# Recurrent gates in three float32r passes, and the last scaling on three engines, in a hybrid RG-LRU and GLA layer

## The chip, the cores and the metric

One core of a Trainium2 chip runs the whole layer in one launch. The metric is the device time of one execution in microseconds (us); the median of three is given. A profiled execution also has a span, from its first instruction to its last. Engines are named as the profile names them: PE (TensorE; PEld is its weight load), DVE (VectorE), ACT (ScalarE), POOL (GpSimd), SP (SyncE, which only issues DMAs here). Each takes its instructions strictly in the order of its own queue and waits at the first whose inputs are missing.

## The reference

One decoder layer for 1024 prompt rows and 8 x 4 sample rows that share the weights. The part that the change touches is the RG-LRU's pair of gates, for ten blocks of 128 channels, and the last RMS norm:

```python
xb = xc.reshape(B, T, LRU_BLOCKS, LRU_BW)
r = sigmoid(einsum('btnw,nwv->btnv', xb, wa) + ba)
i = sigmoid(einsum('btnw,nwv->btnv', xb, wx) + bx)
log_a = -LRU_C * softplus(-lam) * r
b = sqrt(-expm1(2.0 * log_a)) * (i * xc)
h = associative_scan(...)            # h_t = exp(log_a_t) * h_(t-1) + b_t
...
y = x * rsqrt(mean(x * x) + EPS) * final_g
```

Around it stand a GEMM into nine column groups, a causal convolution that gives xc, chunked gated linear attention (GLA), two merging projections, an output projection and a SwiGLU feed-forward network. All is float32.

## The kernel before

Activations lie with 128 features on the partitions and tokens along the columns. The tokens are worked in two halves, one after the other: half A is the first 512 prompt rows, half B the other 512 and the 32 sample rows (544 columns, taken as two pieces of 272). Names end in a for half A and in b for half B (g1a, g1b).

Every large GEMM splits its operands into a rounded float32r part (hi, an ACT copy) and the rest (lo, a DVE subtraction), and `gemm` runs three float32r matmuls for each tile of 128 rows: hi x hi, hi x lo, lo x hi (lines 327 to 329). Weights come by `load_w`: SP loads them into a `raw` buffer (three of them), ACT and DVE split them into an `hl` buffer (three). The gates are the exception. `lru_gate` loads 256 columns of gate weights and runs plain float32 matmuls on them and on xc, one per gate and piece (line 832): g1 for r, g2 for i. ACT then makes tanh of both (tr, ti), an exponential la and a tanh from tr, and a square lm; DVE combines them. `lru` runs over five pairs of blocks. For each it emits `lru_x` (projection ux and convolution, giving xc), `lru_g` of the pair before (projection ug and scan), and then `gate(2b)` and `gate(2b + 1)`.

These generators are interleaved with others by hand: the first pair of half A and the first three of half B stand in the GLA stage, the others among the projections gb and pb of `merge_b`. The order in which this emits the work is a priority, from which a scheduler fixes each engine's queue before the run; it also hands out the buffers of a pool as they come free. Matmul results of half A go to six PSUM buffers of one bank, those of half B to three of two banks. The pool of tag `t`, with six buffers, holds xc, tr, ti and the other short-lived rows.

At the end `finish` scales the last 272 columns. `norm` sums the squares by matmuls (nps, line 334), `rsqrt` does Newton steps on DVE, and `spread` makes a row on all partitions by matmuls (rps, line 346), copied from PSUM by ACT (rb, line 349). Eight DVE instructions (line 1054) give y, and each pair of them is followed by a DMA, from SP's and ACT's queues in turn.

Of the kernel before, what the change touches and what calls it, by code (L numbers as in the profile page):

```python
# [7 lines left out]
F32 = mybir.dt.float32  # L8
F32R = mybir.dt.float32r
I32 = mybir.dt.int32  # L10
AF = mybir.ActivationFunctionType
OP = mybir.AluOpType
# [3 lines left out]
P = 128  # L16
D = 1024
KD = 8
# [13 lines left out]
def starts_of(w):  # L32
    return [min(i, w - P) for i in range(0, w, P)]
# [4 lines left out]
V_BA, V_BX, V_LAM, V_GBA, V_GN, V_FG = 114, 124, 134, 144, 148, 156  # L38
# [4 lines left out]
def bc(ap, shape):  # L43
    return ap.to_broadcast(shape)
# [3 lines left out]
def hybrid_layer(ctx, tc, I, O):  # L48
    nc = tc.nc
    pe, act, dve, pool, sp = nc.tensor, nc.scalar, nc.vector, nc.gpsimd, nc.sync  # L50
# [6 lines left out]
    tp = ctx.enter_context(tc.tile_pool(name="tp", bufs=6))  # L57
    axp = ctx.enter_context(tc.tile_pool(name="axp", bufs=2, space=PSUM))

    def S(name, dt=F32):  # L60
        return sbig.tile([P, 2 * 544], dt, tag="S", name=name)

    def T(name, w=544):
        return tp.tile([P, w], F32, tag="t", name=name)

    def ACC(name):
        return tp.tile([P, 544], F32, tag="acc", name="acc" + name, bufs=2)
# [9 lines left out]
    def mm(name):  # L77
        return mmk[1].tile([P, mmk[0], 512], F32, tag="mm", name=name)

    def ax(name):  # L80
        return axp.tile([P, 512], F32, tag="ax", name=name)
# [4 lines left out]
    vec = cp.tile([P, V_TOT], F32, name="vec")  # L86
# [14 lines left out]
    rmask = cp.tile([P, 544], F32, name="rmask")  # L101
# [13 lines left out]
    def load_raw(src, n, name):  # L115
        raw = wp.tile([P, 1024], F32, tag="raw", name=name + "_raw")
        sp.dma_start(raw[:, :n], src)
        return raw
# [39 lines left out]
    def split(dst, src, n):  # L158
        act.activation(dst[:, 0:n], src, AF.Copy)
        dve.tensor_sub(dst[:, n:2 * n], src, dst[:, 0:n].bitcast(F32))  # L160
# [86 lines left out]
    def rsqrt(dst, ssq, n, scale, name):  # L247
        w = cp.tile([P, 3, 16], F32, name="rs_" + name, tag="rs", bufs=2)
        a, t = w[:, 0, :n], w[:, 1, :n]
        yi = cp.tile([P, 16], I32, name="ri_" + name, tag="ri", bufs=2)  # L250
        dve.tensor_scalar(a, ssq, scale, EPS, op0=OP.mult, op1=OP.add)
        dve.tensor_scalar(yi[:, :n], a.bitcast(I32), -0.5, float(0x5F3759DF), op0=OP.mult, op1=OP.add)
        y = yi[:, :n].bitcast(F32)
        for it in range(3):
            dve.scalar_tensor_tensor(t, a, -0.5, y, op0=OP.mult, op1=OP.mult)
            dve.tensor_mul(t, t, y)
            o = dst if it == 2 else w[:, 2, :n]
            dve.scalar_tensor_tensor(o, t, 1.5, y, op0=OP.add, op1=OP.mult)
            y = o

    def drain(g):
        for _ in g:
            pass
# [25 lines left out]
    class Half:  # L289
# [45 lines left out]
                          start=(first and i == 0), stop=(last and i == len(starts) - 1), skip_group_check=True)  # L335


        def spread(s, rstd, w, name):
            starts = starts_of(w)
            nt = len(starts)  # L340
            rps = [ax("rps" + name)] + ([ax("rpt" + name)] if w > HP else [])
            done = 0
            for i, st in enumerate(starts):
                n = st + P - done
                o = rps[0][:, done:done + n] if done < HP else rps[1][:, :n]
                pe.matmul(o, bc(rstd[:, i:i + 1], [P, P]), ident[:, P - n:], start=True, stop=True)
                done += n
            rb = T("rb" + name)
            act.activation(rb[:, :min(w, HP)], rps[0][:, :min(w, HP)], AF.Copy)
            if w > HP:  # L350
                act.activation(rb[:, HP:w], rps[1][:, :w - HP], AF.Copy)
            return rb

        def add_sq(s, acc, x, w, i, name, apart=False):

# [7 lines left out]
            else:  # L363
                acc.append(sq)

        def norm(s, acc, w, box, name):

            starts = starts_of(w)
            nt = len(starts)
            ps = ax("nps" + name)  # L370
            for i, a in enumerate(acc):
                s.ssq_mm(ps, a, starts, 0, i == 0, i == len(acc) - 1)
            rstd = cp.tile([P, 5], F32, name="rstd" + name, tag="rstd", bufs=2)
            rsqrt(rstd[:, :nt], ps[:, :nt], nt, 1.0 / D, name)
            yield 5
            box.append(s.spread(rstd[:, :nt], w, name))
            yield 1.5

        def modulate(s, hs, xs, rb, part, kts, gslot, sh0, name):
# [446 lines left out]
        def lru_gate(s, nb, m, xc):  # L826
            N, n = s.N, f"{s.n}{nb}"
            gw = load_raw(I["lru_w"][nb], 256, "lw" + n)
            g1, g2 = mm("g1" + n), mm("g2" + n)
            for g, c in (g1, 0), (g2, P):  # L830
                for o, w, bank, off in [(0, HP, 0, 0)] if s.hf == 0 else s.parts:
                    pe.matmul(g[:, bank, off:off + w], gw[:, c:c + P], xc[:, o:o + w], start=True, stop=True)
            tr, ti = T("tr" + n), T("ti" + n)
            act.activation(s.sv(tr[:, :N]), s.pv(g1), AF.Tanh, scale=0.5, bias=vh[:, nb:nb + 1])
            act.activation(s.sv(ti[:, :N]), s.pv(g2), AF.Tanh, scale=0.5, bias=vh[:, 10 + nb:11 + nb])
            dve.scalar_tensor_tensor(ti[:, :N], ti[:, :N], 1.0, xc[:, :N], op0=OP.add, op1=OP.mult)
            a = S("la" + n)
            s4 = sp4[:, nb:nb + 1]
            act.activation(a[:, :N], tr[:, :N], AF.Exp, scale=s4, bias=s4)
            act.activation(tr[:, :N], tr[:, :N], AF.Tanh, scale=s4, bias=s4)  # L840
            act.activation(m, a[:, :N], AF.Square)
            dve.scalar_tensor_tensor(m, m, 1.0, tr[:, :N], op0=OP.add, op1=OP.mult)
            return a, ti
# [198 lines left out]
                    s.add_sq(acc, s.x[j][:, s.cols(part)], w, q, "3" + n, back)  # L1042
                yield w * 33 / 2400.0

        def finish(s, part, acc, queues=(pool,)):
            o, w = part[0], part[1]
            box = []
            yield from s.norm(acc, w, box, f"3{s.n}{o}")
            out = O["y" + s.n].rearrange("p (k n) -> p k n", k=KD)
            for j in range(0, KD, 2):  # L1050
                y = S(f"y{s.n}{o}{j}")
                y2 = y[:, :2 * w].rearrange("p (k n) -> p k n", k=2)
                for i in range(2):
                    dve.scalar_tensor_tensor(y2[:, i], s.x[j + i][:, o:o + w], vec[:, V_FG + j + i:V_FG + j + i + 1], box[0][:, :w],
                                             op0=OP.mult, op1=OP.mult)
                    yield 0.0
                (queues[j // 2 % len(queues)]).dma_start(out[:, j:j + 2, o:o + w], y2)

        def back(s):
            s.x, s.h2 = [], []  # L1060
            p0, p1 = s.parts
            a0, a1 = [ACC("20" + s.n)], [ACC("21" + s.n)]
            drain(s.out_proj(p0, a0))
            o1 = s.out_proj(p1, a1)
            next(o1)
            next(o1)
            mix(s.norm2(p0, a0), o1)
            drain(o1)
            s.act = []
            f = s.ffn1_first(p0, EARLY)  # L1070
            next(f)
            next(f)
            mix(s.norm2(p1, a1), f)
            drain(f)
            drain(s.ffn1_first(p1, EARLY))
            drain(s.ffn1(0, EARLY))
            drain(s.ffn2(0, s.whole))
# [30 lines left out]
    A, B = Half(0), Half(1)  # L1108
# [29 lines left out]
    acc = [ACC("3a")]  # L1138
# [7 lines left out]
    p0, p1 = B.parts  # L1146
    a0, a1 = [ACC("30b")], [ACC("31b")]
# [2 lines left out]
    next(dn)  # L1150
    mix(B.finish(p0, a0), dn)
    drain(dn)
    drain(B.finish(p1, a1, (sp, act)))
    mmp.close()


# [92 lines left out]
```

## Time and profile before

| | |
|---|---|
| median of 3 runs | 2042.66 us (2041.41 to 2043.99) |
| profiled execution | 2046.31 us, span 2044.3 us |
| granted TensorE clock, mean | 0.994 |
| PE busy | 2013.5 us, 98% of the span |
| DVE, ACT, POOL busy | 1097.1, 799.2 and 79.5 us |
| gates of half A | 274 to 438 us of the span |
| gates of half B | 1218 to 1394 us of the span |
| last feed-forward matmul ends | about 2031 us |

In rows of the profile, a timeline row has the start in us, the busy time in us, the engine, the line, the output and inputs, and in brackets how long the engine had been idle and for whom it waited. One plain float32 matmul shows as two PE records. A busy time holds the pipeline's depth, so what a matmul costs in a row of equal ones is read from start to start. A row of a stage (from:to) has its length, the busy time and instruction count of PE, PEld, DVE, ACT and POOL, then the granted clock, the DMA share and GB/s.

### The profile page before, as it was taken

To read this page: it belongs to the slowest core of one execution; us is meant where nothing else is said; L and a number is where in the kernel's file an instruction comes from. 1 tells how busy PE (TensorE), PEld (TensorE's weight loads), DVE (VectorE), ACT (ScalarE), POOL (GpSimd) and SP (SyncE) were. 2 spreads that over 40 slices of the span, in tenths; PEclk is the share of its full clock that TensorE was granted. 3 is DMA by queue.
4 is the path that set the end of the run, shared out by engine and by line. 5 is a ranking of instruction groups with operands and counts; after the bars stand their busy time and mean duration, and the time that the engine had idled before them with its cause. 6 is when DMAs were issued, how large, how long until landed. Compare 5 with 4: busy or idle time off the path is not lost. (4 is left out here: it accounts for less than half of the span.)

```text
span 2044.3 us, 31396 instructions
## 1 busy us (share of the span) xinstructions
PE 2013.5 (98%) x13118; PEld 1811.1 (89%) x13118; DVE 1097.1 (54%) x1768; ACT 799.2 (39%) x1117; POOL 79.5 (4%) x131
## 2 busy tenths in 40 slices
PE   8999999999999999999999999999999999999997
PEld 4777787888899888888899999999999999999997
DVE  4647567654358433446473687774334673333346
ACT  3525356644335322233352455553322442222232
POOL 0101000000000000000010111010000000000000
PEclk9999999999999999999999999999999999999998
DMA  8244423332244323232422312323233542232243
GB/s 304 73 157 149 164 68 100 97 103 87 93 152 158 124 81 115 93 138 79 147 67 92 116 53 93 109 88 104 72 93 106 170 137 92 72 105 90 84 120 123
DMA packets 74637, 228.38 MB, mean 112 GB/s; under 512 B 8704, under 2 KB 16768, under 8 KB 74496
## 3 DMA queue, kind: packets, MB, share of 16 engines
q1 hardware_dynamic: 71536, 217.38, 32.1%
q0 software_dynamic: 2416, 8.44, 1.1%
q8 instruction: 103, 1.69, 0.3%
q10 hardware_dynamic: 544, 0.56, 0.1%
q14 instruction: 38, 0.31, 0.0%
HBM read 217.11 MB, written 9.23 MB: 111 GB/s over the span
## 5 line engine op out<-in xcount | busy, mean ns | idle before, releaser
L329 PE MATMUL f3psb<-fab,f3b_hl 128*128 128x272 f32 x352 | 101.6, 289 | 0.0
L327 PE MATMUL f3psb<-fab,f3b_hl 128*128 128x272 f32 x352 | 101.4, 288 | 0.0
L328 PE MATMUL f3psb<-fab,f3b_hl 128*128 128x272 f32 x352 | 101.0, 287 | 0.0
L124 ACT ACTIVATE f3b_hl<-f3b_raw 128x768 fp32r<-128x768 f32 (+1 forms) x45 | 35.7, 793 | 88.7 <-PE f3psb L329 58.3
L327 PE MATMUL f3psa<-faa,f3a_hl 128*128 128x512 f32 x176 | 68.7, 391 | 0.0
L329 PE MATMUL f3psa<-faa,f3a_hl 128*128 128x512 f32 x176 | 68.6, 390 | 0.0
L328 PE MATMUL f3psa<-faa,f3a_hl 128*128 128x512 f32 x176 | 68.6, 390 | 0.0
L327 PEld LDWEIGHTS f3psb<-fab,f3b_hl 128*128 128x128 f32 x352 | 66.5, 189 | 0.0
L329 PEld LDWEIGHTS f3psb<-fab,f3b_hl 128*128 128x128 f32 x352 | 66.3, 188 | 0.0
L328 PEld LDWEIGHTS f3psb<-fab,f3b_hl 128*128 128x128 f32 x352 | 66.2, 188 | 0.0
L125 DVE TENSOR_TENSOR f3b_hl<-f3b_raw,f3b_hl 128x768 fp32r<-128x768 f32 (+1 forms) x45 | 40.1, 892 | 35.1 <-ACT f3b_hl L124 35.0
L124 ACT ACTIVATE f3a_hl<-f3a_raw 128x768 fp32r<-128x768 f32 (+1 forms) x32 | 25.4, 792 | 84.4 <-PE f3psa L329 46.5
L125 DVE TENSOR_TENSOR f3a_hl<-f3a_raw,f3a_hl 128x768 fp32r<-128x768 f32 (+1 forms) x32 | 28.5, 892 | 39.1 <-ACT f3a_hl L124 38.5
L327 PE MATMUL uxpsb<-h1b,uxpsb_hl 128*128 128x272 f32 x160 | 47.6, 298 | 0.1
L329 PE MATMUL uxpsb<-h1b,uxpsb_hl 128*128 128x272 f32 x160 | 46.7, 292 | 0.0
L328 PE MATMUL uxpsb<-h1b,uxpsb_hl 128*128 128x272 f32 x160 | 46.2, 289 | 0.0
L327 PE MATMUL ugpsb<-h1b,ugpsb_hl 128*128 128x272 f32 x160 | 46.2, 289 | 0.0
L329 PE MATMUL ugpsb<-h1b,ugpsb_hl 128*128 128x272 f32 x160 | 46.2, 289 | 0.0
L328 PE MATMUL ugpsb<-h1b,ugpsb_hl 128*128 128x272 f32 x160 | 45.9, 287 | 0.0
L329 PEld LDWEIGHTS f3psa<-faa,f3a_hl 128*128 128x128 f32 x176 | 33.0, 188 | 7.1 <-DVE f3a_hl L125 0.2
L328 PEld LDWEIGHTS f3psa<-faa,f3a_hl 128*128 128x128 f32 x176 | 33.1, 188 | 6.9
L327 PEld LDWEIGHTS f3psa<-faa,f3a_hl 128*128 128x128 f32 x176 | 33.1, 188 | 6.6
(1478 smaller groups left out, 7149.0 us busy)
## 6 DMA issues: line engine op xcount, KB each, us to landing
ada<-in_ada_w SPq DMA_DIRECT2D x48, 512.0 KB, 5.4
f3b_raw<-in_ffn SPq DMA_DIRECT2D x23, 384.0 KB, 3.1
f3b_raw<-in_ffn SPq DMA_DIRECT2D x22, 320.0 KB, 2.8
woa_raw<-in_w_out SPq DMA_DIRECT2D x13, 512.0 KB, 3.4
wob_raw<-in_w_out SPq DMA_DIRECT2D x13, 512.0 KB, 3.3
f3a_raw<-in_ffn SPq DMA_DIRECT2D x16, 384.0 KB, 3.1
uxpsa_raw<-in_w_in SPq DMA_DIRECT2D x10, 512.0 KB, 3.7
ugpsa_raw<-in_w_in SPq DMA_DIRECT2D x10, 512.0 KB, 3.5
```

Of the source, the lines that this page charges most:

```text
L124: act.activation(hl[:, 0, :n], raw[:, :n], AF.Copy)
L125: dve.tensor_sub(hl[:, 1, :n], raw[:, :n], hl[:, 0, :n].bitcast(F32))
L327: pe.matmul(out, wh, x[:, o:o + w], start=st, stop=False)
L328: pe.matmul(out, wh, x[:, N + o:N + o + w], start=False, stop=False)
L329: pe.matmul(out, wl, x[:, o:o + w], start=False, stop=en)
```

## The change

The gates: each block's gate weights are split into gs (hi in columns 0 to 255, lo in 256 to 511), a new tile with one buffer, and xc into xh (ACT) and xl (DVE), tiles of the pool `t`. Each plain matmul becomes three float32r ones: hi x hi, hi x lo, lo x hi. The raw weights are read by the split and no longer by PE.

The end: for the last 272 columns only (`end=True`), two plain matmuls of 512 columns on `rmask` are put between nps and rps; the scaling on DVE reads the row from PSUM (rps) where it read the copy rb; and the last pair of the eight tiles (j = 6) goes first, scaled by the gain on ACT and by rb on POOL.

```diff
@@ -335,7 +335,7 @@
                           start=(first and i == 0), stop=(last and i == len(starts) - 1), skip_group_check=True)
 
 
-        def spread(s, rstd, w, name):
+        def spread(s, rstd, w, name, both=False):
             starts = starts_of(w)
             nt = len(starts)
             rps = [ax("rps" + name)] + ([ax("rpt" + name)] if w > HP else [])
@@ -349,7 +349,7 @@
             act.activation(rb[:, :min(w, HP)], rps[0][:, :min(w, HP)], AF.Copy)
             if w > HP:
                 act.activation(rb[:, HP:w], rps[1][:, :w - HP], AF.Copy)
-            return rb
+            return (rb, rps[0]) if both else rb
 
         def add_sq(s, acc, x, w, i, name, apart=False):
 
@@ -363,7 +363,7 @@
             else:
                 acc.append(sq)
 
-        def norm(s, acc, w, box, name):
+        def norm(s, acc, w, box, name, between=None):
 
             starts = starts_of(w)
             nt = len(starts)
@@ -373,7 +373,9 @@
             rstd = cp.tile([P, 5], F32, name="rstd" + name, tag="rstd", bufs=2)
             rsqrt(rstd[:, :nt], ps[:, :nt], nt, 1.0 / D, name)
             yield 5
-            box.append(s.spread(rstd[:, :nt], w, name))
+            if between is not None:
+                box.append(between())
+            box.append(s.spread(rstd[:, :nt], w, name, between is not None))
             yield 1.5
 
         def modulate(s, hs, xs, rb, part, kts, gslot, sh0, name):
@@ -826,10 +828,19 @@
         def lru_gate(s, nb, m, xc):
             N, n = s.N, f"{s.n}{nb}"
             gw = load_raw(I["lru_w"][nb], 256, "lw" + n)
+            gs = tp.tile([P, 512], F32R, tag="gs", name="gs" + n, bufs=1)
+            split(gs, gw[:, :256], 256)
+            xh, xl = (tp.tile([P, 544], F32R, tag="t", name=u + n) for u in ("xh", "xl"))
+            act.activation(xh[:, :N], xc[:, :N], AF.Copy)
+            dve.tensor_sub(xl[:, :N], xc[:, :N], xh[:, :N].bitcast(F32))
             g1, g2 = mm("g1" + n), mm("g2" + n)
             for g, c in (g1, 0), (g2, P):
+                wh, wl = gs[:, c:c + P], gs[:, 256 + c:256 + c + P]
                 for o, w, bank, off in [(0, HP, 0, 0)] if s.hf == 0 else s.parts:
-                    pe.matmul(g[:, bank, off:off + w], gw[:, c:c + P], xc[:, o:o + w], start=True, stop=True)
+                    out = g[:, bank, off:off + w]
+                    pe.matmul(out, wh, xh[:, o:o + w], start=True, stop=False)
+                    pe.matmul(out, wh, xl[:, o:o + w], start=False, stop=False)
+                    pe.matmul(out, wl, xh[:, o:o + w], start=False, stop=True)
             tr, ti = T("tr" + n), T("ti" + n)
             act.activation(s.sv(tr[:, :N]), s.pv(g1), AF.Tanh, scale=0.5, bias=vh[:, nb:nb + 1])
             act.activation(s.sv(ti[:, :N]), s.pv(g2), AF.Tanh, scale=0.5, bias=vh[:, 10 + nb:11 + nb])
@@ -1042,19 +1053,31 @@
                     s.add_sq(acc, s.x[j][:, s.cols(part)], w, q, "3" + n, back)
                 yield w * 33 / 2400.0
 
-        def finish(s, part, acc, queues=(pool,)):
+        def finish(s, part, acc, queues=(pool,), end=False):
+
             o, w = part[0], part[1]
             box = []
-            yield from s.norm(acc, w, box, f"3{s.n}{o}")
+            yield from s.norm(acc, w, box, f"3{s.n}{o}", s.stay_busy if end else None)
+            rb, rp = box[-1] if end else (box[0], box[0])
             out = O["y" + s.n].rearrange("p (k n) -> p k n", k=KD)
-            for j in range(0, KD, 2):
+            for j in (6, 0, 2, 4) if end else range(0, KD, 2):
                 y = S(f"y{s.n}{o}{j}")
                 y2 = y[:, :2 * w].rearrange("p (k n) -> p k n", k=2)
                 for i in range(2):
-                    dve.scalar_tensor_tensor(y2[:, i], s.x[j + i][:, o:o + w], vec[:, V_FG + j + i:V_FG + j + i + 1], box[0][:, :w],
-                                             op0=OP.mult, op1=OP.mult)
+                    x, g = s.x[j + i][:, o:o + w], vec[:, V_FG + j + i:V_FG + j + i + 1]
+                    if end and j == 6:
+                        act.activation(y2[:, i], x, AF.Copy, scale=g)
+                        pool.tensor_mul(y2[:, i], y2[:, i], rb[:, :w])
+                    else:
+                        dve.scalar_tensor_tensor(y2[:, i], x, g, rp[:, :w], op0=OP.mult, op1=OP.mult)
                     yield 0.0
                 (queues[j // 2 % len(queues)]).dma_start(out[:, j:j + 2, o:o + w], y2)
+
+        def stay_busy(s):
+            ps = mm("busy" + s.n)[:, 0]
+            for _ in range(2):
+                i = pe.matmul(ps, rmask[:, :P], rmask[:, :512], start=True, stop=True, skip_group_check=True)
+                tc.keep_in_program_order(i)
 
         def back(s):
             s.x, s.h2 = [], []
@@ -1150,7 +1173,7 @@
     next(dn)
     mix(B.finish(p0, a0), dn)
     drain(dn)
-    drain(B.finish(p1, a1, (sp, act)))
+    drain(B.finish(p1, a1, (sp, act), True))
     mmp.close()
```

The third pair of gates of half A (blocks 4 and 5), in PE's queue. Before (pbpsa and gbpsa are the GEMMs around it; the numbers tell buffers apart):

```order
L329 MATMUL pbpsa_2595<-yba_2298,pba_hl 128x512
L832 MATMUL g1a_2630<-xca_2434,lwa_raw 128x512
L832 MATMUL g2a_2631<-xca_2434,lwa_raw 128x512
L832 MATMUL g1a_2646<-xca_2548,lwa_raw 128x512
L832 MATMUL g2a_2647<-xca_2548,lwa_raw 128x512
L327 MATMUL gbpsa_2661<-h1a_244,gbpsa_hl 128x512
```

And now:

```order
L841 MATMUL g1a_2681<-xha_2677,gsa_2674 128x512
L842 MATMUL g1a_2681<-xla_2678,gsa_2674 128x512
L843 MATMUL g1a_2681<-xha_2677,gsa_2674 128x512
L841 MATMUL g2a_2682<-xha_2677,gsa_2674 128x512
L842 MATMUL g2a_2682<-xla_2678,gsa_2674 128x512
L843 MATMUL g2a_2682<-xha_2677,gsa_2674 128x512
L841 MATMUL g1a_2708<-xha_2704,gsa_2701 128x512
L842 MATMUL g1a_2708<-xla_2705,gsa_2701 128x512
L843 MATMUL g1a_2708<-xha_2704,gsa_2701 128x512
L841 MATMUL g2a_2709<-xha_2704,gsa_2701 128x512
L842 MATMUL g2a_2709<-xla_2705,gsa_2701 128x512
L843 MATMUL g2a_2709<-xha_2704,gsa_2701 128x512
```

Six matmuls stand where two stood for each block, those of the second block (2708, 2709) directly behind those of the first, and the next GEMM behind both.

The same place in ACT's queue before (gga and yaa belong to `lru_g`, ugpsa_hl is a weight split):

```order
L124 ACTIVATE uxpsa_hl<-uxpsa_raw 128x1024
L851 ACTIVATE gga_2583<-gga_2583 128x512
L159 ACTIVATE yaa_2592<-gga_2583 128x512
L834 ACTIVATE tra_2634<-g1a_2630,vh 128x512
L124 ACTIVATE ugpsa_hl<-ugpsa_raw 128x1024
L835 ACTIVATE tia_2635<-g2a_2631,vh 128x512
L839 ACTIVATE laa_2639<-tra_2634,sp_107 128x512
L834 ACTIVATE tra_2650<-g1a_2646,vh 128x512
L840 ACTIVATE tra_2634<-tra_2634,sp_107 128x512
L841 ACTIVATE lma_2627<-laa_2639 128x512
```

And now, where xha_2704 and gsa_2701 are the second block's:

```order
L862 ACTIVATE gga_2627<-gga_2627 128x512
L834 ACTIVATE xha_2677<-xca_2478 128x512
L159 ACTIVATE yaa_2636<-gga_2627 128x512
L124 ACTIVATE ugpsa_hl<-ugpsa_raw 128x1024
L845 ACTIVATE tra_2689<-g1a_2681,vh 128x512
L846 ACTIVATE tia_2690<-g2a_2682,vh 128x512
L850 ACTIVATE laa_2694<-tra_2689,sp_107 128x512
L159 ACTIVATE gsa_2701<-lwa_raw 128x256
L851 ACTIVATE tra_2689<-tra_2689,sp_107 128x512
L852 ACTIVATE lma_2671<-laa_2694 128x512
L834 ACTIVATE xha_2704<-xca_2592 128x512
L845 ACTIVATE tra_2716<-g1a_2708,vh 128x512
```

The weight split ugpsa_hl has moved ahead of the first block's tra, gs of the second block stands behind the first block's laa, and the second block's xh behind its lma.

The end of POOL's queue, which before ended with the four DMAs:

```order
L1074 DMA out_yb<-yb_18173 128x2x272
L1074 DMA out_yb<-yb_18177 128x2x272
L1074 DMA out_yb<-yb_18181 128x2x272
L1074 DMA out_yb<-yb_18185 128x2x272
L1070 TENSOR_TENSOR yb_18473<-yb_18473,rb3b_18471 128x272 x2
```

The two multiplications are new; in ACT's queue the two products with the gain stand some ten instructions ahead of the end, and the DMA of the j = 6 pair ahead of that of j = 2.

## Prediction

> **What bounds the kernel now.** I read the page's first part, then who waited for whom on PE, then the timeline around the gates, then clock windows.
>
> ```profile
> PE 2013.5 (98%) x13118; PEld 1811.1 (89%) x13118; DVE 1097.1 (54%) x1768; ACT 799.2 (39%) x1117; POOL 79.5 (4%) x131
> PE spsb L620 <- DVE wb L611: 2.3, 1, 2.3
> PE g1b L832 <- DVE mbb L921: 1.0, 1, 1.0
> ```
>
> PE is busy for 98% of the span and its longest wait inside is 2.3 us, so PE's queue is the kernel: matmul time taken away is time won, and each new wait in that queue is time lost, since PE has no slack in which to catch up. ACT and DVE are half empty, but only on average. What matters is when they hand their results to PE. The third pair of gates of half A shows that stage:
>
> ```profile
> 337.16 0.58 ACT L916 ACTIVATE gba<-gbpsa 128x512 f32<-128x512 f32 x1
> 351.73 0.68 DVE L852 SCALAR_TENSOR_TENSOR gga<-gga,ugpsa 128x512 f32<-128x512 f32 x1
> 352.31 1.02 PE L832 MATMUL g1a<-xca,lwa_raw 128*128 128x512 f32 x2
> 352.45 0.69 DVE L867 SCALAR_TENSOR_TENSOR gga<-laa,gga 128x512 f32<-128x512 f32 x1
> 353.17 1.02 PE L832 MATMUL g2a<-xca,lwa_raw 128*128 128x512 f32 x2
> 353.17 0.63 ACT L159 ACTIVATE yaa<-gga 128x512 fp32r<-128x512 f32 x1 [2.10 <-DVE gga L867]
> 353.83 0.69 DVE L160 TENSOR_TENSOR yaa<-gga,yaa 128x512 fp32r<-128x512 f32 x1 [0.69 <-ACT yaa L159]
> 355.42 1.06 ACT L124 ACTIVATE ugpsa_hl<-ugpsa_raw 128x1024 fp32r<-128x1024 f32 x1 [1.05 <-DMA ugpsa_raw<-in_w_in]
> 356.44 0.39 PE L327 MATMUL gbpsa<-h1a,gbpsa_hl 128*128 128x512 f32 x1
> 356.96 0.81 ACT L839 ACTIVATE laa<-tra,sp 128x512 f32<-128x512 f32 x1
> 357.12 0.39 PE L327 MATMUL gbpsa<-h1a,gbpsa_hl 128*128 128x512 f32 x1
> 357.67 0.67 ACT L834 ACTIVATE tra<-g1a,vh 128x512 f32<-128x512 f32 x1
> 358.23 0.81 ACT L840 ACTIVATE tra<-tra,sp 128x512 f32<-128x512 f32 x1
> 358.94 0.62 ACT L841 ACTIVATE lma<-laa 128x512 f32<-128x512 f32 x1
> 359.46 0.68 ACT L835 ACTIVATE tia<-g2a,vh 128x512 f32<-128x512 f32 x1
> 359.60 0.69 DVE L842 SCALAR_TENSOR_TENSOR lma<-lma,tra 128x512 f32<-128x512 f32 x1 [1.25 <-ACT lma L841]
> 360.03 0.81 ACT L839 ACTIVATE laa<-tra,sp 128x512 f32<-128x512 f32 x1
> ```
>
> Today both gates of the pair go through PE from 352.31 on without a break, and the ACT rows of the gates (356 to 361) run beside the next GEMM. Nothing that PE does here waits for them.
>
> **The change part by part.**
>
> *Fewer passes.* A plain matmul of 512 columns takes 0.86 us start to start (352.31 to 353.17). Three float32r ones take 0.68 (356.44 to 357.12, one L327 to the next). 20 such matmuls in half A: 20 x 0.18 = 3.6 us less. For half B:
>
> ```profile
> 1216.24 0.40 ACT L802 ACTIVATE ubb<-uxpsb 128x272 f32<-128x272 f32 x1 [3.82 <-PE uxpsb L329]
> 1216.53 0.36 ACT L803 ACTIVATE ubb<-uxpsb 128x240 f32<-128x240 f32 x1
> 1344.21 1.08 PE L832 MATMUL g1b<-xcb,lwb_raw 128*128 128x272 f32 x4
> 1345.12 1.08 PE L832 MATMUL g2b<-xcb,lwb_raw 128*128 128x272 f32 x4
> 1349.52 0.29 PE L327 MATMUL gbpsb<-h1b,gbpsb_hl 128*128 128x272 f32 x1
> 1349.89 0.29 PE L327 MATMUL gbpsb<-h1b,gbpsb_hl 128*128 128x272 f32 x1
> ```
>
> Two plain ones take 0.91, so 0.455 each, against 0.37 for three passes: 40 x 0.085 = 3.4 us. Together 7.0 us, about 0.7 a pair.
>
> *The splits.* Each gate adds two ACT copies and two DVE subtractions, off PE. ACT and DVE could carry the sum. But gs has one buffer, so the second gate's gs may be written only when PE has read the first gate's for the last time, and in ACT's new order its gs and xh stand behind work that needs the first gate's results: tra, tia, laa, **gs**, tra, lma, **xh**. In PE's order the second gate's six matmuls stand right behind the first's six, with the next GEMM behind them. PE therefore stands still until that chain is through. From the end of the first gate's g1, start to start by the rows above: tra 0.56 (357.67 to 358.23), tia 0.57 (359.46 to 360.03), laa 0.71 (356.96 to 357.67), gs 0.30 (256 columns; nearest is 1216.24 to 1216.53), tra 0.71, lma 0.52, then xh 0.60 (nearest the yaa row of the same form, 0.63): 3.97 us, and 0.06 each for two hand-offs, 4.1. Beside it lies only g2 (0.46 to 0.68), so PE idles 3.5 us. Then xl: DVE first does lma (0.69, starting when ACT's lma is done, as xh starts), then the subtraction (0.69): ready 0.85 after xh, of which one pass covers 0.23 to 0.46: 0.5 more.
>
> *The clock.* An idle PE also loses its clock:
>
> ```profile
> 1182.00:1183.00 1.00, 0.00 (x0) 0.00 (x0) 1.00 (x3) 0.17 (x1) 0.00 (x0) 1.00 0.00 0
> 1183.00:1184.00 1.00, 0.00 (x0) 0.00 (x0) 1.00 (x3) 1.00 (x2) 0.00 (x0) 0.93 0.00 0
> 1186.00:1187.00 1.00, 1.00 (x5) 0.98 (x5) 1.00 (x2) 0.88 (x2) 0.00 (x0) 0.50 0.00 0
> 1187.00:1188.00 1.00, 1.00 (x9) 1.00 (x8) 1.00 (x2) 0.66 (x1) 0.00 (x0) 0.87 0.00 1
> 1346.00:1347.00 1.00, 0.20 (x1) 0.00 (x0) 1.00 (x2) 0.97 (x3) 0.00 (x0) 1.00 0.36 33
> ```
>
> After the 2.3 us wait the granted clock (the column behind POOL) stands at 0.50 from about 1183.9 to 1187.3, some 3.4 us; after the 1.0 us wait it stays at 1.00. A wait of 3.5 us is nearer to the first. The price lies between 0 and 1.7 us (half of 3.4). I take 1.2, because part of the slow stretch falls on the wait for xl.
> The Trainium skill, "TensorE: Matmul & The Clock Gate", section "Why this matters for your kernels", wants no PE gaps above about 3 us. The 2.3 us row shows that less already does it. By that rule the two or three pairs with divided waits would pay nothing and the sum would be some 3 us less; I go by the row.
>
> So a pair of half A costs 3.5 + 0.5 + 1.2 - 0.7 = 4.5 us. To this comes: in pairs 1, 3 and 5 the first gate's xl is late too (DVE is in gga until 352.4, xl at 353.1, while PE is through its first pass at 352.54): 0.5. In pairs 3 and 5 yaa, now behind that xl, and a weight split (1.06) stand ahead of tra: 1.9. In pairs 2 and 4 gba (0.58, which reads the GEMM that has just ended) stands ahead of the first xh (0.6): PE waits 1.2 before the pair, and 0.3 for xl. Half A: 22.5 + 0.5 + 2 x 2.4 + 2 x 1.5 = 30.8 us.
>
> In half B the chain is 544 wide (about 4.2), the second wait is partly filled (0.3): 4.4 a pair. There gla's matmuls fill some waits, each ups taking 0.44:
>
> ```profile
> 272.36 0.60 PE L677 MATMUL upsa<-va,kta 128*128 128x256 f32 x2
> 272.80 0.61 PE L675 MATMUL poa<-qea,sta 128*128 128x128 f32 x4
> ```
>
> Pair 1 has four ups between its gates (-1.7) but a first xl that waits behind DVE's cv and copies (+1.3): 4.0. Pair 2 has three ups and eleven short po matmuls (3.7 us by these rows) there, so wait and slow clock nearly vanish: 0.5. Pair 3 has the rps, which themselves wait for rstd, against a yab in the chain: 4.2. Pair 4: a split ahead of tra costs 1.0, but the 1.0 us wait of today goes: 4.4. Pair 5: gbb and a split ahead, as in pairs 2 and 4 of A: 6.3. Half B: 19.4 us.
>
> SP issues as many DMAs as before; the first gate's raw buffer comes free earlier, at the split, and that hides no new work of PE's.
>
> **The end.**
>
> ```profile
> 2009.74 0.57 PE rps3b L346 x6
> 2035.35 1.46 PE L346 MATMUL rps3b<-ident,rstd3b 128*128 128x128 f32 x6 [2.22 <-DVE rstd3b L258]
> 2036.85 0.40 ACT L349 ACTIVATE rb3b<-rps3b 128x272 f32<-128x272 f32 x1 [4.60 <-PE rps3b L346]
> 2037.28 3.39 DVE L1054 SCALAR_TENSOR_TENSOR yb<-xmb,vec,rb3b 128x272 f32<-128x272 f32 x8 [1.99 <-ACT rb3b L349]
> L557 POOL TENSOR_TENSOR qea<-qa,e0a 128x1024 f32<-128x1024 f32 x2 | 4.8, 2386 | 150.5 <-DMA ada<-in_ada_w 98.1 <-ACT e0a L556 52.4
> ```
>
> From rps to the last yb are 3.86 us now (2036.81 to 2040.67). DVE no longer waits for rb (-0.4) and does six of eight (-0.84): 2.6. POOL waits for rb and multiplies twice; 2.39 us for 1024 columns gives 0.63 for 272 (up to 0.9), so yb's last pair is ready at 1.8 to 2.3, and ACT's queue issues it ahead of another: 2.6 to 3.3 in all, a gain of 0.6 to 1.3. The two added matmuls on rmask take four times 0.43 between nps and rps. If they keep the clock, rps takes 0.57 instead of 1.46 (-0.9); if the clock is gone in spite of them, they run at half of it, past rstd (+0.7). I take -1.0 for the end, with bounds of -2.2 and +0.1.
>
> **Sum.** 30.8 + 19.4 - 1.0 = +49 us on the profiled execution's 2046.31 us: 2095.5. That execution stands 3.65 us above the median of the runs shown, so 2092 against 2042.66.
>
> **Rivals.**
> (a) *Faster.* The waits vanish, as in pair 2 of half B, because PE has queued work between the two gates, or because the copies come early. The point is 3.5 us of PE work between the halves of a pair. Then 7.0 + 1.0 remain: 2034.7. For it speaks only that ACT is idle 2.10 us ahead of yaa, time in which an xh fits; against it PE's order, where nothing stands between, and the one buffer of gs.
> (b) *Shorter waits.* The clock holds, the extra items ahead of tra cost nothing, and the chain is a fifth shorter: -11, -10 and -7, so +21 and 2064.
> (c) *Longer ones.* Each wait falls across two clock stretches and the full 1.7 us or more is paid: +14, 2106.
> (d) *No effect.* Waits just eat the 7 us: 2042. It would take 0.7 us a pair, a sixth of the chain.
>
> **Chances.** Forecast (2075 to 2100) 0.60, (b) 0.18, (c) 0.13, (a) 0.06, (d) 0.03. The range 2062 to 2108 leaves out (a), (d) and the tails of (b) and (c). Faster or slower by over 0.2%, which is about what a measurement of this kernel can tell from no change: faster 0.06, slower 0.91, within 0.03.
>
> **What would show it.** PE's waits list g1a and g1b behind ACT xh (about 3.5 us a pair) and behind DVE xl (0.5); PE's busy share falls to some 96%; the granted clock falls below 1.00 ten times in the two stages of the gates; six f32r passes take 1.4 us where the clock is whole; the first yb starts right behind rps. I am wrong if PE shows no waits of over 2 us at the gates, or if ACT's xh of the second gate is done before the first gate's g2.

## The result, and the profile after

The changed kernel takes 2110.38 us (median of four runs, 2108.8 to 2111.22) against 2042.16 for the kernel before on the same chip: ratio 1.0327, 95% interval 1.0312 to 1.0341. It is slower, as forecast, but by 68 us and not by 49. Its profiled span is 2109.4 us, 65.1 more than before.

The page's first part, and who waited for whom on PE (total us, times, longest):

```profile
PE 2034.1 (96%) x13182; PEld 1828.8 (87%) x13182; DVE 1118.6 (53%) x1806; ACT 818.0 (39%) x1159; POOL 81.0 (4%) x133
PE g1a L841 <- ACT xha L834: 24.4, 7, 5.0
PE g1b L841 <- ACT xhb L834: 9.4, 4, 3.7
PE opsb L334 <- DVE oacb L753: 3.6, 1, 3.6
PE rpsob L346 <- DVE orstdb L258: 3.4, 1, 3.4
PE spsb L622 <- DVE attb L637: 1.9, 1, 1.9
PE g1a L842 <- DVE xla L835: 1.7, 4, 0.8
```

The gates wait for xh, as the prediction said. The third pair of half A, whose rows before it showed, now reads:

```profile
371.77 0.39 PE L843 MATMUL g2a<-xha,gsa 128*128 128x512 f32 x1
371.80 0.67 ACT L845 ACTIVATE tra<-g1a,vh 128x512 f32<-128x512 f32 x1
372.37 0.68 ACT L846 ACTIVATE tia<-g2a,vh 128x512 f32<-128x512 f32 x1
372.94 0.81 ACT L850 ACTIVATE laa<-tra,sp 128x512 f32<-128x512 f32 x1
373.64 0.41 ACT L159 ACTIVATE gsa<-lwa_raw 128x256 fp32r<-128x256 f32 x1
373.95 0.80 ACT L851 ACTIVATE tra<-tra,sp 128x512 f32<-128x512 f32 x1
374.66 0.62 ACT L852 ACTIVATE lma<-laa 128x512 f32<-128x512 f32 x1
375.18 0.62 ACT L834 ACTIVATE xha<-xca 128x512 fp32r<-128x512 f32 x1
375.85 0.80 PE L841 MATMUL g1a<-xha,gsa 128*128 128x512 f32 x1 [3.69 <-ACT xha L834]
376.65 0.80 PE L842 MATMUL g1a<-xla,gsa 128*128 128x512 f32 x1
377.25 0.63 PE L843 MATMUL g1a<-xha,gsa 128*128 128x512 f32 x1
377.67 0.63 PE L841 MATMUL g2a<-xha,gsa 128*128 128x512 f32 x1
378.10 0.63 PE L842 MATMUL g2a<-xla,gsa 128*128 128x512 f32 x1
```

This is the chain of seven that the prediction named, in its order, and a wait of 3.69 us where it said 3.5. What it under-read comes next: after the wait the passes start 0.43 us apart (377.25, 377.67, 378.10), where a pass at the full clock takes 0.23.

Two stages hold the whole loss. Half A's is taken from the first matmul of qa to the first of gapsa, half B's from the first of uxpsb to the first of gapsb; behind the bounds stand the length, PE's busy time, the granted clock. Before:

```profile
74.40:482.30 407.90, 405.45 (x2035) 1.00 0.33 114
1201.80:1472.30 270.50, 266.74 (x2065) 0.99 0.28 93
```

After:

```profile
72.70:519.10 446.40, 416.98 (x2055) 0.96 0.31 105
1238.70:1537.50 298.80, 276.06 (x2105) 0.96 0.25 82
```

That is +38.5 us in half A (forecast 30.8) and +28.3 in half B (19.4). From the start of the last feed-forward matmul to the end of the span it takes 14.2 us, 13.6 before (forecast 1.0 less). The rest of the program is unchanged within 2 us.

### The profile page after: what moved, and what is told of

Read it like the earlier page. It is cut to its first block, busy times and chain, and to the rows that moved or that the text cites. A ratio compares the mean times of both kernels' runs of the same rounds, so it can differ in the third digit from the quotient of the medians.

```text
span 2109.4 us, 31648 instructions
## 1 busy us (share of the span) xinstructions
PE 2034.1 (96%) x13182; PEld 1828.8 (87%) x13182; DVE 1118.6 (53%) x1806; ACT 818.0 (39%) x1159; POOL 81.0 (4%) x133
## 4 chain that ended last, share of the span: by engine, by line
PE 90%; DVE 5%; ACT 3%; issue 1%; DMA 0%; POOL 0%; DVEq 0%; SPq 0%; ACTq 0%; POOLq 0%
PE f3psb L327 2%; PE f3psb L329 2%; PE f3psb L328 2%; PE f3psa L327 2%; PE f3psa L329 2%; PE f3psa L328 2%; PE adaps L186 1%; PE spsa L622 1%; PE spsb L622 1%; PE papsb L327 1%; PE papsb L329 1%; PE papsb L328 1%; PE uxpsa L327 1%; PE uxpsb L327 1%; PE uxpsa L329 1%
```

## Experiments

Each run was timed beside the kernel before on the same chip, and ratios are to it. "Stage" means the two stretches above. How long the clock stood at 0.50 is read from windows of 1 us. Where the gates are those of before, half B's stage took 268.9, 270.5, 270.8 and 272.5 us in the profiles (e9, before, e11, e3). The clock stood at 0.50 for 0, 3.4, 3.4 and 6.8 us of them, so one stretch of 3.4 us goes with 1.6 to 1.9 us more, and a difference of 2 us there says nothing about an edit.

### The added work alone (e1), and the two parts of the change apart (e2, e3)

```diff
 # e1, in lru_gate: gs, xh, xl made and left unread; end of before
-                    pe.matmul(out, wh, xh[:, o:o + w], start=True, stop=False)
-                    pe.matmul(out, wh, xl[:, o:o + w], start=False, stop=False)
-                    pe.matmul(out, wl, xh[:, o:o + w], start=False, stop=True)
+                    pe.matmul(g[:, bank, off:off + w], gw[:, c:c + P], xc[:, o:o + w], start=True, stop=True)
 # e2 (and e1): the end of before, as follows; e3 keeps the new end and has the gates of before
-    drain(B.finish(p1, a1, (sp, act), True))
+    drain(B.finish(p1, a1, (sp, act)))
```

> The parts gs, xh and xl are made as in the changed kernel, but nothing reads them: the gates are the plain f32 matmuls of before, and the end is that of before. Theory 1 (PE waits because the gates' passes stand behind xh, made late on ACT): no gate waits, 2042 to 2046 us. Rival 4 (the added ACT and DVE work delays everything by itself): more than half of the 68 us stays, above 2076.

Measured: 1.0018 (1.0009 to 1.0028). No gate waits for parts, half A's stage is 408.0 us as before; half B's is 274.4. The 18.6 us of ACT and 20.5 us of DVE work that this kernel has more than before (817.8 and 1117.6 busy) cost about 4 us, 2 to 6 by the interval. So the rival "the work itself" is not the cause of the 68 us: what costs is that PE needs the results in time.

> The f32r gates with the end of before. By the trace of the changed kernel the new end is worth about +0.5 us, so 2109 to 2110.5 us; by the prediction's sum it was worth -1.0, so 2111.4. If the new end is what the forecast lacked, 2092 to 2100.

Measured: 1.0319 (1.0303 to 1.0334), stages 445.5 and 299.8: the gates are the whole loss.

> The gates of before with the new end. By the trace +0.5 us: 2042.7; by the prediction's sum -1.0: 2041.2. All theories have it within 2 us of 2042.2; the profile's last 12 us decide.

Measured: 0.9994 (0.9985 to 1.0004). The end brings nothing; its 14.2 us stand against 13.6.

### Which buffer holds xh back (e5, e6, e7)

```diff
 # e5: gs gets two buffers
-            gs = tp.tile([P, 512], F32R, tag="gs", name="gs" + n, bufs=1)
+            gs = tp.tile([P, 544], F32R, tag="acc", name="gs" + n, bufs=2)[:, :512]
 # e6: xh gets two buffers of its own
-            xh, xl = (tp.tile([P, 544], F32R, tag="t", name=u + n) for u in ("xh", "xl"))
+            xh = tp.tile([P, 544], F32R, tag="acc", name="xh" + n, bufs=2)
+            xl = tp.tile([P, 544], F32R, tag="t", name="xl" + n)
 # e7: e6's xh, and gs in two tiles, gh (hi) and gl (lo)
+            gh = tp.tile([P, 256], F32R, tag="gh", name="gh" + n, bufs=2)
+            gl = tp.tile([P, 256], F32R, tag="gl", name="gl" + n, bufs=1)
...
```

> The changed kernel with two buffers for the split weights gs (they lie in the idle tag acc); xh and xl stay in the pool t. Theory 1 as the prediction had it (the one gs buffer puts the second gate's xh behind the first gate's ACT chain): the waits between the gates go, 2045 to 2060 us. Rival 3 (xh and xl wait for buffers of t by themselves): xh still stands behind tr, ti and la, 0.56 + 0.57 + 0.71 + 0.60 = 2.4 us in place of 3.5, so about 1.1 less for each of ten pairs, 2096 to 2104 us.

> The changed kernel with two buffers of its own for xh (the idle tag acc); gs keeps one. Theory 1: the second gate's weight split stands behind the whole ACT chain, so 3.4 us between the gates as before; what goes is only the wait for xh ahead of the first gate (5.0 and 1.2 us in half A's pairs 2 and 4): 2098 to 2106 us. Rival 3 (t alone orders it): 2045 to 2060.

> Two buffers for xh and two for the upper part of the weights; xl stays in t, the lower part of the weights keeps one buffer. If both buffers together were the cause, no wait for xh between the gates is left; xl, behind the first gate on DVE, makes 0.5 to 1.5 us of wait per pair: 2050 to 2070 us. If the waits are those of the ACT work itself, above 2085.

Measured: e5 1.0239 (1.0222 to 1.0256), 2092.9 us; e6 1.022 (1.0204 to 1.0237), 2090.5; e7 1.0049 (1.0034 to 1.0064), 2055.0. PE's waits in e5:

```profile
PE g1a L841 <- ACT xha L834: 16.3, 7, 4.6
PE g1b L841 <- ACT xhb L834: 8.8, 5, 2.6
```

and in e6 (L842 is there the pass hi x hi, L843 hi x lo):

```profile
PE g1a L842 <- ACT gsa L159: 10.6, 5, 2.9
PE g1a L843 <- DVE xla L836: 7.6, 3, 6.4
PE g1b L842 <- ACT gsb L159: 6.2, 3, 2.4
```

In e5 the pairs still wait for xh, 2.0 to 2.2 us between the gates in half A. It lies in `t` there; that it needs the very buffer which the first gate's passes free is argued from the pool's six buffers, no row names it. In e6, with xh out of `t`, the list names no xh. The pairs wait for gs instead (1.9 to 2.9 us between the gates in half A), and pair 2's first gate waits 6.4 us for an xl that stands behind eight subtractions for yb in DVE's queue. By the ratios each edit alone gives back 18 and 22 us, both together 57. The prediction's one cause, gs, was one of two. In e7 half A takes 408.9 us, about as before; what it still loses lies in half B (279.4).

e5 and e6 ended 3 and 8 us below what was expected of them. Those expectations counted waits, and the slow clock went with the waits: in half A it stood at 0.50 for 34.1 us in the changed kernel, for 17.1 in e5 and 20.5 in e6. In e6 the waits between the gates were also shorter than the 3.4 us that its expectation took.

### What the clock costs (e8)

```diff
                 gate(2 * b)
+                if s.hf == 0:
+                    s.fill(b)
...
+        def fill(s, b):
+            ps = mm(f"fill{s.n}{b}")[:, 0]
+            for _ in range(3):
+                i = pe.matmul(ps, rmask[:, :P], rmask[:, :512], start=True, stop=True, skip_group_check=True)
+                tc.keep_in_program_order(i)
```

> The changed kernel with three plain f32 matmuls (0.86 us each) between the two gates of each pair of half A, which nothing reads: the wait for xh stays as long, but TensorE works for 2.6 of its 3.6 us. What is left of the loss is the wait alone. Theory 2 (the clock lost after each wait costs 2 us or more, not the 1.2 of the sum): 7 to 11 us less, 2099 to 2103. By the prediction's 1.2: 2104 to 2106. If the clock is nothing: 2110. Half A's stage, 519.1 us at its end, tells it without half B.

Measured: 1.0273 (1.0257 to 1.0288), 2099.9 us. The third pair:

```profile
367.86 2.74 PE L1081 MATMUL filla<-rmask 128*128 128x512 f32 x6
371.70 0.50 PE L841 MATMUL g1a<-xha,gsa 128*128 128x512 f32 x1 [1.10 <-ACT xha L834]
372.04 0.40 PE L841 MATMUL g2a<-xha,gsa 128*128 128x512 f32 x1
```

Half A's stage:

```profile
72.60:508.10 435.50, 420.35 (x2086) 0.99 0.32 107
```

PE reaches the second gate no earlier: from the start of the first gate's last pass it is 4.08 us in both kernels (367.62 to 371.70, 371.77 to 375.85). But the passes behind run at the full clock, and the stage is 10.9 us shorter; half B's, left alone, is 299.2, 298.8 in the changed kernel. From pair 3's second gate to pair 4's first it is 40.96 us against 43.66, from pair 4's second gate to pair 5's 44.81 against 46.84 (0.3 of that by a wait for xl). So a wait of 3.6 us costs 1.7 to 2.7 us more by the clock. Over half A's stage PE was at work at 0.50 for some 25 us in the changed kernel and for some 7 in e8. Half of the difference, about 9 of the 10.9 us, is clock; the rest is not told apart (in e8 two passes of gb also stand ahead of the second gate's first pass that needs xl). In the changed kernel the slow clock reaches past the gates, as pair 3's windows show (the first holds the wait):

```profile
370.00:380.00 10.00, 6.30 (x19) 0.72 0.40 134
380.00:390.00 10.00, 10.00 (x43) 0.94 0.09 20
```

### Both gates' parts made ahead (e4), and where that pays (e9, e10, e12)

```diff
 # e4, in lru; gate_parts splits into hl[:, nb % 2, :512], xh lies in tag acc, xl in t, which has 7 buffers
+                hl = wp.tile([P, 2, 1024], F32R, tag="hl", name=f"lw{s.n}{b}_hl", bufs=3)
+                for nb in (2 * b, 2 * b + 1):
+                    xp_[nb] = s.gate_parts(nb, hl, xs[nb])
                 gate(2 * b)
 # e9, in gate_parts: half B's gates as before (e12: "if nb < 4"); both with the end of before
+            if s.hf:
+                return gw, xc, None
 # e10 (new end, as e4)
-            dve.tensor_sub(xl[:, :N], xc[:, :N], xh[:, :N].bitcast(F32))
+            (pool if s.hf else dve).tensor_sub(xl[:, :N], xc[:, :N], xh[:, :N].bitcast(F32))
```

> The changed kernel, but both gates' parts are made ahead of the first gate's passes: their weights share one hl tile, xh has two buffers of its own and the pool t has seven. Theory 1: the waits for xh between a pair's gates go, with the slow clock behind them, and the fewer passes show: 68 us back and about 4.6 us for each half below that, 2033 to 2040 us. Rival 2 (the clock is lost to waits for DVE and ACT work in half B too, which stay): 2050 to 2065. Rival 4 (the added work itself): above 2076.

Measured: 1.0037 (1.0024 to 1.005). On the 2042.2 us of before that is 2049.7, just below rival 2's range and well above theory 1's. Its stages:

```profile
72.50:480.40 407.90, 402.91 (x2056) 1.00 0.34 114
1200.20:1478.70 278.50, 269.76 (x2106) 0.98 0.28 90
```

Half A is back at 407.9 us: the waits for xh are gone (0.3 left) and the clock is whole. The passes do save 0.69 us a pair (2.74 from a pair's first pass to the next GEMM's first, 3.43 before), 3.5 in all, of which small new waits of 2.5 us (1.3 of them for yb, ahead of a pb) take most. Half B keeps 8 us. Its longest waits there:

```profile
PE opsb L334 <- DVE oacb L753: 2.0, 2, 1.8
PE spsb L622 <- DVE attb L637: 1.6, 1, 1.6
```

These are GLA's, not the gates'. They fall among half B's first three pairs, where the gates and GLA share the stage. PE's waits in the stage are 5.0 us longer than before in sum (8.6 against 3.6). The clock stands at 0.50 for 13.7 us, beginning at these two waits, against 3.4 before, which costs about 5 more. Less the 3.4 that half B's passes should save, that is 6.6 of the 8 us.

> Half A's gates in f32r with both gates' parts made ahead (as in e4), half B's gates in f32 as before, the end of before. If the 8 us that e4 keeps are due to half B's added parts: half B's stage takes 270 to 272 us as before, half A's 408, and the time is that of before within 0.2% (ratio 0.998 to 1.002). If they are due to e4's other buffers or to half A: 2048 to 2052, ratio 1.002 to 1.004.

Measured: 0.9999 (0.9988 to 1.0011); stages 407.8 and 268.9. The 8 us belong to half B's f32r gates.

> e4 with half B's xl made by GpSimd in place of DVE: ten subtractions of 0.68 us leave DVE, and take about 1.5 us each on GpSimd (272 columns took 0.74 there). If e4's rest in half B is DVE's queue behind the added work: 3 to 6 us less than e4, ratio to before 1.001 to 1.002. If not, or if the gates wait for GpSimd: as e4 or slower, 1.004 to 1.008.

Measured: 1.0024 (1.0013 to 1.0034). Its half B's stage is 277.7, 0.8 less than e4's: taking xl off DVE (1.35 us each on GpSimd) is not what decides there. The ratio is lower than e4's, but the two intervals overlap.

> As e9, with the f32r gates only in pairs 3 to 5, of both halves, where e9 and e4 show no gate waiting; pairs 1 and 2 have their f32 gates, the end is that of before. If a pair saves what its passes are fewer by (3.43 us of f32 against 2.74 of f32r, 0.69), six pairs save 4.1 us: ratio to before 0.998, 0.997 to 0.999. If the seventh buffer of t or the added ACT and DVE work gives it back: 1.000 to 1.002.

Measured: 0.9995 (0.9986 to 1.0004); stages 406.2 and 272.3. Half A keeps 1.7 of the 2.1 us that its three pairs save; half B's 272.3 lies at the top of the spread of unchanged gates, so most of e4's 8 us go with the f32r gates of pairs 1 and 2. In e12 sps no longer waits; ops still waits 1.85 us, and the clock stands at 0.50 for 6.8 us from there on. Why the DVE results for these two come late was not tried. The saving expected is not shown by the time. No version tried is measurably faster than the kernel before.

### The end without its two matmuls (e11)

```diff
         def stay_busy(s):
-            ps = mm("busy" + s.n)[:, 0]
-            for _ in range(2):
-                i = pe.matmul(ps, rmask[:, :P], rmask[:, :512], start=True, stop=True, skip_group_check=True)
-                tc.keep_in_program_order(i)
+            pass
```

> The gates of before and the new end without its two plain matmuls. By the trace of e3 (14.2 us from the last f3psb pass's start to the end, 13.6 before) they hold rps back past rstd: 0.5 us less, 13.6 to 13.8. By the prediction they keep the clock for rps: 0.5 us more, 14.5 or longer.

Measured once: 2044.64 us, beside 2044.78. From the last feed-forward residual (DVE on xmb) to the first yb it takes 6.28 us, 6.69 in e3 and 6.29 before: the two matmuls cost 0.4. From the last feed-forward matmul's start to the end it is 13.8 us, against 14.2 with them and 13.6 before. In the changed kernel's timeline:

```profile
2097.55 3.17 PE L1079 MATMUL busyb<-rmask 128*128 128x512 f32 x4
2099.69 0.16 DVE L258 SCALAR_TENSOR_TENSOR rstd3b<-rs_3b 128x3 f32<-128x3 f32 x1
2100.52 1.25 PE L346 MATMUL rps3b<-ident,rstd3b 128*128 128x128 f32 x6
2101.80 0.40 ACT L349 ACTIVATE rb3b<-rps3b 128x272 f32<-128x272 f32 x1 [5.00 <-PE rps3b L346]
2102.23 2.54 DVE L1072 SCALAR_TENSOR_TENSOR yb<-xmb,vec,rps3b 128x272 f32<-128x272 f32 x6 [2.38 <-ACT rb3b L349]
```

They run past rstd and rps is still slow; DVE still starts behind ACT's rb, though it no longer reads it (why was not tried). Its work for y is 0.85 us shorter, and yet the end comes 7.2 us after the first yb, 7.0 before. The output's queues say why. Transfers of the 10 us from 2036 on in the kernel before, with packets, MB and their time as a share of all 16 engines:

```profile
q1 hardware_dynamic: 544, 0.56, 16.4%
q10 hardware_dynamic: 544, 0.56, 16.0%
```

and in the changed kernel, from 2101 on:

```profile
q10 hardware_dynamic: 544, 0.56, 16.2%
q1 hardware_dynamic: 544, 0.56, 15.9%
```

Both take 3.2 us of all 16 engines for the same 1.12 MB, and while they run the engines are full: a share of 0.95 to 1.06 in windows of 0.5 us, but for the first and the last. The first output DMA is issued 0.93 to 0.94 us after the first yb begins, in both. From there the transfers are the bound, and a DVE that is done earlier only queues them.

## Why the prediction was right or wrong

*Right.* The direction, the mechanism and its place: PE waits for the second gate's xh behind that ACT chain, 3.53 to 3.69 us in each of half A's five pairs (said: 3.5). The passes: 0.69 us a pair at the full clock (said: 0.7). Half A's waits in sum: 26.9 us of new ones in the timeline against 28.3 worked out.

*Wrong: the price of the clock.* The term of 1.2 us a pair was mis-sized. Half A lost 38.5 us; less 26.9 of waits, and with the 3.5 that the passes save, 15.1 are left, 3.0 a pair, against 5 x 1.2 = 6. In half B the waits rose from 3.6 to 22.6 us; by the same working 12.7 are left, against some 5. The two together are 17 us over, and the miss of both stages is 66.8 - 50.2 = 16.6.

Most of what is left is the slow clock, as the granted clock shows. It fell ten times in the two stages, as was said, but each time it stayed at 0.50 for 3.4, 6.8 or 13.7 us: 34.1 us in half A and 23.9 in half B, where it had been none and 3.4. PE was at work for some 25 and 23 of these, and half of that time is lost: about 12 us in half A, and about 10 more than before in half B. The other 5 to 6 us of the two remainders no row assigns. Pair 2 had the longest fall:

```profile
320.00:330.00 10.00, 4.67 (x8) 0.50 0.34 102
330.00:340.00 10.00, 10.00 (x38) 0.83 0.01 5
```

For half A e8 shows it by an edit: filling only the waits between the gates won 10.9 us, some 9 of them by the clock; pair 2's other waits were not filled. For half B no run did that. The step that failed is the choice within 0 to 1.7: its ceiling came from one stretch of 3.4 us, and half A's five pairs had ten such stretches. Part of them did fall on waits, as the discount had it, but mostly on those for xh; the waits for xl between the gates were at most 0.3. Rival (c), 2106, which had each wait fall across two stretches, came nearest.

*Wrong within a right sum.* The yaa and the weight split ahead of tra in pairs 3 and 5 (1.9 each) cost little: tra began 0.3 us after g1's last pass had ended, and the waits there, 3.69, are no more than 0.16 above the other pairs'. The first gate's late xl (0.5 in pairs 1, 3 and 5) cost 0.3 in pair 1 and nothing in the others. Ahead of pair 2 PE waited 5.0 us and not 1.2, because eight splits of yb stood in ACT's queue too:

```profile
315.70 4.25 ACT L159 ACTIVATE yba<-sra 128x512 fp32r<-128x512 f32 x8
319.86 0.57 ACT L927 ACTIVATE gba<-gbpsa 128x512 f32<-128x512 f32 x1
320.34 0.62 ACT L834 ACTIVATE xha<-xca 128x512 fp32r<-128x512 f32 x1
```

That half A's waits came out near their sum is therefore partly luck. In half B the gates wait for xh 9.4 us in all, where 3.5 and more for each of four pairs were worked out, while ops, rps and sps, matmuls of GLA, wait 8.9 for DVE results that none of the steps had. At these three waits begin 17.1 of the 23.9 us of slow clock.

*Wrong: the cause named for the chain.* "The one buffer of gs" holds only together with the pool `t` (e5 to e7). The point of rival (a), copies that come early, is real: e4 makes them early and half A's loss is gone. But then 0.69 us a pair is all there is to win.

*Wrong: the end.* -1.0 was forecast, +0.6 came, beyond the bound of +0.1. Three terms failed: the two matmuls do not keep the clock and cost 0.4 (the prediction had this as its bad case, at 0.7), DVE still waits for rb (said -0.4), and the shorter DVE work (-0.84, measured -0.85) is lost to the transfers.

## What to carry to other kernels

Where one engine is 98% busy, a conversion that saves it passes must have its operands ready one step ahead. Count every tile that the conversion allocates, and ask for each whether its buffer is freed by the very instructions that wait: here two such tiles had to be freed together. Price a wait of PE by the wait and the slow clock behind it, and find the transfer behind the last instruction before shortening that one. Then ask what there is to win: here 0.69 us a pair, and no version won it measurably.

## What was not expected of the hardware

A wait of 3.6 us cost PE 1.7 to 2.7 us more in passes at 0.43 us; three unread 0.86 us matmuls in the wait, which left 1.1 us idle, avoided that (e8). Shorter pauses do it too: in e4's half B GLA's sps, behind a wait of 1.57 us,

```profile
1220.40 3.67 PE L622 MATMUL spsb<-wb 128*128 128x64 f32 x16 [1.57 <-DVE attb L637]
```

takes twice what it took without one before:

```profile
1229.63 1.90 PE L620 MATMUL spsb<-wb 128*128 128x64 f32 x16
```

The length of a pause alone does not decide it. In the kernel before, the clock stood at 0.50 from 1303.3 to 1306.7 behind no wait above 0.5 us: from 1299.5 on PE had run twenty ops matmuls of a single column, between waits of 0.25 and 0.49. Behind a wait of 1.14 us at 1240 it stayed whole.

At the end of the changed kernel the clock fell while PE was busy. PE was at work for 0.22 us of 2096 to 2097, and the clock fell more than a microsecond later, under the two full matmuls:

```profile
2096.00:2097.00 1.00, 0.22 (x3) 1.00 0.00 0
2097.00:2098.00 1.00, 1.00 (x7) 1.00 0.00 0
2098.00:2099.00 1.00, 1.00 (x3) 0.58 0.00 0
2099.00:2100.00 1.00, 1.00 (x3) 0.50 0.00 0
```

So the two matmuls, which start after the pause, came too late to save the clock. Matmuls of a single column (nps) stand around the pause here too, and the runs do not tell their part from the pause's. The Trainium skill, "TensorE: Matmul & The Clock Gate", section "Part 1: The HAM clock gate", has the gate watch a free-running window of about 3.4 us; a fall that comes after the pause agrees with that, while its wait of at least one idle window does not agree with the 1.57 us above.
